# Two transformer blocks in one kernel: key and query products issued by array shape, and expert weights loaded one matrix at a time

## The chip, the core and the metric

The kernel runs on one core of a Trainium2 chip. The metric is the device time of one execution, in microseconds. Before the change it is 2284.15 us, the median of three runs (2281.66 to 2285.14).

In what follows PE is the matrix engine, DVE the vector engine, ACT the scalar engine, POOL the GpSimd engine and SP the queue that issues the loads. A matmul keeps one operand (the weights, at most 128 rows by 128 columns) in the array and streams the other one past it. "64 rows" below means that the contraction runs over 64 partitions, so that the matmul uses half of the array's rows; "64 columns" means that its output has 64 partitions.

## What is computed

512 tokens of width 1024 go through two blocks, all in float32:

```python
# first block
h   = rms_norm(x, ln1_g);  proj = h @ w_in
attn = neighbourhood_attention(rms_norm(q), rms_norm(k), v, rpb)   # 8 heads of 64
dn   = bidirectional_gated_deltanet(...)                           # 4 heads of 128, both directions
x = x + concat(attn, dn) @ w_out
x = x + hierarchical_moe(rms_norm(x, ln2_g), ...)                  # 64 experts, 2 per token
# an expert:  hid = silu(xb @ w_gate[e]) * (xb @ w_up[e]);  out = hid @ w_down[e]

# second block
proj = rmsnorm(x) @ w_in_2
y = three branches: mlstm, short_conv, stick_breaking              # the last: 16 heads of 64
# stick_breaking, per head:
z = q @ k.T / 8;  log_beta = log_sigmoid(z);  log_1m = where(s < t, log_beta - z, 0)
a = where(s < t, exp(log_beta + log_1m.sum() - cumsum(log_1m)), 0);  out = a @ v
x = x + merged @ w_out;  x = x + relu(rmsnorm(x) @ w_up)**2 @ w_down
return rmsnorm(x)
```

## The kernel before

Most products go through jobs: a weight tile of 1 MB is loaded into ring A (two buffers), ACT and DVE split it into a high and a low half (lines 160 and 161), and PE multiplies (high, high), (high, low) and (low, high), 24 matmuls of 128 rows, 128 columns and 512 streamed columns a job (`fm_mm`, line 255). The profile prints such operands as f32 too; they take one pass, and a true float32 matmul takes two records, one for each half of its weights.

Where nothing else is said, the framework schedules each engine's order from its own costs. In the expert loop and in the stick-breaking stage PE's order is written out by hand (`manual_schedule`).

**Neighbourhood attention** (about 264 to 361 us of the span). `na_attn` goes over 4 blocks of queries and 4 pairs of heads; `na_pair` (line 727) does one pair. For each head `i` of the pair it takes one PSUM tile `na_l` from the pool `pacc` (four banks), multiplies q by k (line 743: 64 rows, 256 or 384 streamed columns, the first head on partitions 0 to 63, the second on 64 to 127), adds the mask through an identity matrix `idb` (line 747: 128 rows, bf16), and lets DVE add the bias and take the maximum (line 750). The pair's turn is cut by `yield`s, between which `pad` lets the chunked scan of the delta rule (`dn_scan`) go on.

**Experts** (about 477 to 965 us). `moe` goes over 32 pairs of experts. Loads are queued in the order of `moe_loads` into rings of 1 MB tiles (A, B, C, H, O), and each takes its tile when one is free. `ld_gu` (line 1150) fills one tile with half `h` of an expert's gate and up matrices: two loads of 512 KB, each partition reading 4 KB in a row. `ld_down` (line 1159) fills a tile with one load of 1 MB, 8 KB in a row. `gate_up` (line 1441) then runs 8 steps `k`; in each, for both experts (output columns 0 to 63 and 64 to 127 of the array), one matmul streams 512 columns, 256 of gate and 256 of up. Between its first and second half stand the products of the pair before with the down matrix (`dn_o`, line 1482); behind it come the gather of the next tokens (`g_ps`, line 1426), and at the start of a pair the transposes `h_ps` (line 1464). The string `"ggaaaaggaaaa"` runs four steps of `gate_up` ahead of the first release of two tiles.

**Stick breaking** (about 1041 to 1295 us). `sb_pair` (line 1858) does two heads, `e` = 0 and 1, eight times over, between the dense jobs. Scores lie in three PSUM banks a head, `z[e][0..2]`, six of the pool `pat`'s six; the four regions `REG` have 512, 384, 256 and 128 columns. Per region and head stand one matmul of 128 rows (line 1868: `K` holds a head's rounded keys twice, `Q` its queries' high and low halves) and one of 64 rows (line 1870: `Kl`, the rest of the keys, on partitions 0 to 63 for head 0 and 64 to 127 for head 1). Then the mask is added through `idr` (line 1875), ACT and DVE compute the logarithms, and triangular and all-ones constants (`ntri`, line 1904; `none`, lines 1908 to 1913) sum them up on PE. The output `po` (`sb_o`, line 1923) takes a seventh tile of the pool, and `split_y` (lines 1682 and 1683) copies it out through ACT and then DVE.

**Constants**: `oner` and `none` are one column of ones and minus ones, read 128 times over with step 0 (`b2_consts`, line 1681); `oner` serves the mLSTM heads.

Of the kernel before, what the change touches and what calls it, by code (L numbers as in the profile page):

```python
# [10 lines left out]
F32 = mybir.dt.float32  # L11
# [70 lines left out]
class Kern:  # L82
# [648 lines left out]
    def na_pair(self, cb, g, block, po, sm):  # L731
# [4 lines left out]
        v = lambda a: a.rearrange("p (r k) -> p r k", r=8)  # L736
        for i in range(2):
            h = 2 * g + i
            hp, o = h // 2, 64 * (h % 2)
            lp = na.tile([128, 384], F32, name="na_lp", tag="na_lp", bufs=3)[:, :nb * 128]  # L740
            pl = self.pacc.tile([128, 384], F32, name="na_l", tag=self.atag)[:, :nb * 128]

            TE.matmul(pl, self.qT[o:o + 64, hp, cb, :],
                      self.kT[o:o + 64, hp, kb0 * 128:(kb0 + nb) * 128]
                      .rearrange("p (n r k) -> p r n k", n=nb, r=8), start=True, stop=False)
            mk = self.mk[:, None, s0:s0 + st * (nb - 1) + 1:st, :].to_broadcast([128, 8, nb, 16])
            TE.matmul(pl, self.idb, mk, start=False, stop=True)
            base = self.braw[:, h, 16 * (kb0 - cb + 1):16 * (kb0 - cb + 1) + 1]
            bias = bass.AP(tensor=base.tensor, offset=base.offset, ap=[list(base.ap[0]), [31, 8], [1, 16 * nb]])
            VE.tensor_tensor_reduce(out=v(lp), in0=v(pl), in1=bias, scale=1.0, scalar=NEG,  # L750
                                    op0=OP.add, op1=OP.max, accum_out=mx[:, i:i + 1])
            lps.append(lp)
            if i == 0:
                yield 0.3 * nb
# [395 lines left out]
    def ld_gu(self, t, e, h):  # L1150

        for i, nm in enumerate(("gate", "up")):
            src = self.A["expert_w_" + nm][e]
            if len(src.shape) == 3:
                src = src.rearrange("o r c -> (o r) c")
            self.SY.dma_start(t.rearrange("p (i j c) -> p i j c", i=2, j=4)[:, i],
                              src.rearrange("(p j) c -> p j c", j=8)[:, 4 * h:4 * h + 4, :])
# [6 lines left out]
    def moe_loads(self):  # L1164
        us = []
        for p in range(33):
            if p:
                us += [lambda t, e=2 * p - 2 + e: self.ld_down(t, e) for e in range(2)]
            if p < 32:
                us += [lambda t, e=2 * p + e, h=h: self.ld_gu(t, e, h) for h in range(2) for e in range(2)]  # L1170
# [271 lines left out]
    def gate_up(self, pool, xt, pp, w):  # L1442
# [3 lines left out]
        for k in range(8):  # L1446
            for e in range(2):
                o = pp * 128 + e * 64
                TE.matmul(pg[64 * e:64 * e + 64, :], xt[k // 4][:, k % 4, o:o + 64],  # L1449
                          w[k // 4 * 2 + e].rearrange("p (i j c) -> p i j c", i=2, j=4)[:, :, k % 4, :],  # L1450
                          start=(k == 0), stop=(k == 7))
            if k < 7:
                yield
# [50 lines left out]
    def moe(self):  # L1504
# [14 lines left out]
        with tc.manual_schedule(engines={mybir.EngineType.PE}):  # L1519
            hd, adds = None, iter(())  # L1520
            for p in range(33):
# [20 lines left out]
                for n in "ggaaaaggaaaa":  # L1542
# [649 lines left out]
```

## Time and profile before

| | |
|---|---|
| median of three runs | 2284.15 us (2281.66 to 2285.14) |
| profiled execution | 2290.18 us, of which 2288.4 us are the span of the trace |
| PE busy | 2196.5 us, 96% of the span, 11333 matmul records |
| DVE, ACT, POOL busy | 999.3, 783.0, 146.0 us |
| moved by DMA | 348.71 MB, 152 GB/s over the span; 405 GB/s between 515 and 944 us |

A row of a list of windows gives the stretch in us from the start of the span, its length, the busy time and the count of instructions of PE, of PE's weight loads (PEld), DVE, ACT and POOL, then the granted PE clock (1.00 is full), the busy share of the 16 DMA engines, and GB/s. A row of the timeline gives start, length, engine, line, operation, what is written from what, and the shape: "64*128 64x512" is 64 rows, 128 columns, 512 streamed columns. Matmuls are pipelined, so the time that one takes in a stream is read from start to start, not from its length. In a list of one line's instructions the three numbers are the shortest, the median and the longest in ns.

### The profile page before, as it was taken

Reading aid. Unit: us, or ns where it says so; the run is one execution under the profiler, and the core shown is the slowest. Engines: PE = TensorE matmul, PEld = TensorE weight load, DVE = VectorE, ACT = ScalarE, POOL = GpSimd, SP = SyncE. Lnnn points to the kernel's source line nnn. Section 1 sums busy time; section 2 is a strip of 40 time slices with the busy share of each in tenths; the row PEclk is TensorE's granted clock in tenths of the full one; section 3 lists DMA queues with packets and bytes.
Section 4 is the critical chain, followed back from the end, with each engine's and each line's share of the span. In section 5 each row is a group of like instructions: output and inputs, shape, how many; then the busy total and the mean of one; then the engine's idle time right before and its main releaser. Section 6 shows DMA issues by size and latency. Waiting matters only on the chain.

```text
span 2288.4 us, 27538 instructions
## 1 busy us (share of the span) xinstructions
PE 2196.5 (96%) x11333; PEld 1659.2 (73%) x11333; DVE 999.3 (44%) x1622; ACT 783.0 (34%) x1245; POOL 146.0 (6%) x171
## 2 busy tenths in 40 slices
PE   6989999899999999779999999999999999999998
PEld 4867787755555555357777788888888888888887
DVE  5479667521111111253555444555344444534333
ACT  3545543211111111134565524444322342423222
POOL 1020001000000000011122000000000000000000
PEclk9999999999999999888999999999999999999999
DMA  6212100789999999912111222222233322323322
GB/s 186 73 57 74 57 2 19 268 283 413 412 410 412 399 394 409 351 56 63 56 43 51 74 75 79 81 79 74 92 102 99 104 92 83 111 92 98 105 92 74
DMA packets 175397, 348.71 MB, mean 152 GB/s; under 512 B 15604, under 2 KB 115037, under 8 KB 167075
## 3 DMA queue, kind: packets, MB, share of 16 engines
q1 hardware_dynamic: 169827, 339.25, 41.6%
q0 software_dynamic: 4592, 4.50, 0.6%
q10 hardware_dynamic: 848, 3.15, 0.4%
q8 instruction: 91, 1.49, 0.3%
q14 instruction: 39, 0.32, 0.0%
HBM read 336.61 MB, written 22.02 MB: 157 GB/s over the span
## 4 chain that ended last, share of the span: by engine, by line
PE 56%; DVE 1%; ACT 0%; issue 0%; DMA 0%; POOLq 0%; POOL 0%; ACTq 0%
PE acc L255 37%; PE acc L305 8%; PE acc L332 2%; PE acc L214 2%; PE sb_z L1870 1%; PE sb_z L1868 1%; PE sb_o L1923 1%; PE sb_z L1904 1%; PE ml_s L2045 1%; PE ml_pn L2065 1%; PE pv L1825 0%; PE sb_z L1908 0%; PE n_ps L443 0%; PE sb_z L1875 0%; PE ml_pd L2065 0%; PE sb_z L1912 0%
## 5 line engine op out<-in xcount | busy, mean ns | idle before, releaser
L255 PE MATMUL acc<-hT,hl_fm 128*128 128x512 f32 x3504 | 829.9, 396 | 2.1 <-DVE hl_fm L161 2.0
L255 PEld LDWEIGHTS acc<-hT,hl_fm 128*128 128x128 f32 x3504 | 660.7, 190 | 142.8 <-issue 3.8
L161 DVE TENSOR_TENSOR hl_fm<-rawA,hl_fm 128x1024 fp32r<-128x1024 f32 x176 | 217.4, 1235 | 145.8 <-ACT hl_fm L160 145.6
L160 ACT CAST hl_fm<-rawA 128x1024 fp32r<-128x1024 f32 x176 | 184.6, 1050 | 269.4 <-PE acc L255 201.1
L1449 PE MATMUL gu<-rawB,XT 128*64 128x512 f32 x528 | 186.2, 609 | 12.8 <-DMA rawB<-in_expert_w_up_dram 12.5
L305 PE MATMUL acc<-hl_tm,uT 128*128 128x512 f32 x672 | 152.8, 389 | 0.0
L305 PEld LDWEIGHTS acc<-hl_tm,uT 128*128 128x128 f32 x672 | 126.1, 188 | 26.2
L1457 DVE TENSOR_TENSOR hd<-sg,gu 128x256 f32<-128x256 f32 x32 | 13.5, 421 | 274.8 <-ACT sg L1455 274.8
L1426 PEld LDWEIGHTS g_ps<-oneh,h 128*128 128x128 f32 x960 | 115.5, 188 | 23.6 <-issue 16.2
L1426 PE MATMUL g_ps<-oneh,h 128*128 128x256 f32 x960 | 121.7, 284 | 0.0
L1449 PEld LDWEIGHTS gu<-rawB,XT 128*64 128x64 f32 x528 | 57.9, 139 | 82.6 <-issue 72.2
L1485 ACT ACTIVATE obs<-dn_o,slots 128x512 f32<-128x512 f32 x60 | 41.2, 687 | 194.5 <-PE dn_o L1482 188.1
L1482 PE MATMUL dn_o<-rawB,ht 128*64 128x512 f32 x280 | 102.3, 605 | 1.6 <-DVE x L1501 1.6
L1449 PE MATMUL gu<-rawH,XT 128*64 128x512 f32 x208 | 94.3, 596 | 1.3 <-DMA rawH<-in_expert_w_up_dram 0.8
L161 DVE TENSOR_TENSOR hl_tm<-rawA,hl_tm 128x1024 fp32r<-128x1024 f32 x48 | 58.8, 1224 | 67.2 <-ACT hl_tm L160 67.1
L255 PE MATMUL acc<-yA,hl_fm 128*128 128x512 f32 x384 | 87.4, 389 | 0.0
L255 PEld LDWEIGHTS acc<-yA,hl_fm 128*128 128x128 f32 x384 | 72.1, 188 | 15.0
L160 ACT CAST hl_tm<-rawA 128x1024 fp32r<-128x1024 f32 x48 | 50.3, 1048 | 95.2 <-PE acc L305 86.4
L305 PE MATMUL acc<-hl_tm,hT 128*128 128x512 f32 x288 | 74.6, 413 | 0.0
L1449 PE MATMUL gu<-rawC,XT 128*64 128x512 f32 x152 | 70.5, 605 | 1.2 <-DMA rawC<-in_expert_w_up_dram 1.1
L305 PEld LDWEIGHTS acc<-hl_tm,hT 128*128 128x128 f32 x288 | 55.5, 198 | 11.1
L1440 ACT ACTIVATE XT<-g_ps,g 128x256 f32<-128x256 f32 x64 | 26.8, 470 | 106.0 <-PE g_ps L1426 100.6
(511 smaller groups left out, 2931.6 us busy)
## 6 DMA issues: line engine op xcount, KB each, us to landing
rawA<-in_w_in_dram SPq DMA_DIRECT2D x66, 1024.0 KB
rawB<-in_expert_w_down_dram SPq DMA_DIRECT2D x35, 1024.0 KB
rawB<-in_expert_w_gate_dram SPq DMA_DIRECT2D x66, 512.0 KB
rawB<-in_expert_w_up_dram SPq DMA_DIRECT2D x66, 512.0 KB
rawA<-in_w_up_dram SPq DMA_DIRECT2D x16, 1024.0 KB
rawA<-in_w_down_dram SPq DMA_DIRECT2D x16, 1024.0 KB
rawH<-in_expert_w_down_dram SPq DMA_DIRECT2D x13, 1024.0 KB
rawH<-in_expert_w_gate_dram SPq DMA_DIRECT2D x26, 512.0 KB
```

The source lines that it names most:

```text
L160: self.SE.copy(hi, src)
L161: self.VE.tensor_sub(lo, src, hi.bitcast(F32))
L214: self.TE.matmul(p[:, t:t + 256], j[4][:, a, k, :], h[:, b, k, t:t + 256], start=(t == 0 and i == 0), stop=(t > 0 and i == 23), skip_group ...
L255: self.TE.matmul(ps, hl[:, a, k, :], h[:, b, k, :], start=(n == 0), stop=(n == 23))
L305: self.TE.matmul(ps, h[:, a, k, c * 128:(c + 1) * 128], hl[:, b, kk, :], start=(first and n == 0), stop=(last and n == 5))
L332: self.TE.matmul(ps, h[:, a, k, c * 128:(c + 1) * 128], st["w"][:, b, k, :], start=(n == 0), stop=(n == 23))
L1426: TE.matmul(ps[:, k % 2, :], self.h2[:, a, c, k * 128:(k + 1) * 128], oh[:, c].rearrange("p e s -> p (e s)"), start=(n == 0), stop=(n == 7))
L1440: self.SE.activation(xt[:, 2 + j, :], ps[:, j, :], AF.Copy, scale=self.g2[:, 2 * i + j:2 * i + j + 1])
L1449: TE.matmul(pg[64 * e:64 * e + 64, :], xt[k // 4][:, k % 4, o:o + 64], w[k // 4 * 2 + e].rearrange("p (i j c) -> p i j c", i=2, j=4)[:, :, ...
L1482: TE.matmul(po[64 * e:64 * e + 64, :], ht[:, j, 64 * e:64 * e + 64], w[e].rearrange("p (j c) -> p j c", j=2)[:, j, s], start=(j == 0), sto ...
L1485: SE.activation(ob[:, s], po, AF.Copy, scale=sl[:, 1:2])
L1868: TE.matmul(z[e][b][:, c:c + n], K[:, e, ks], Q[:, e, i * 128:512], start=(i != 3), stop=False, skip_group_check=True)
```

## The change

It edits four places. In `na_pair` both heads' q by k products are issued first and both masks after them, with one `yield` behind both instead of one between the heads. In `sb_pair` the eight matmuls of 128 rows come first and the eight of 64 rows after them. `ld_gu` loads one whole matrix, gate or up, with one load of 1 MB (8 KB in a row for each partition), and `gate_up` runs 16 steps of 256 streamed columns, the 8 of gate ahead of the 8 of up. `oner` and `none` become full tiles of 128 by 128.

```diff
+        pls = [self.pacc.tile([128, 384], F32, name="na_l", tag=self.atag)[:, :nb * 128] for _ in range(2)]
+        for i in range(2):
+            o = 64 * i
+            TE.matmul(pls[i], self.qT[o:o + 64, g, cb, :],
+                      self.kT[o:o + 64, g, kb0 * 128:(kb0 + nb) * 128]
+                      .rearrange("p (n r k) -> p r n k", n=nb, r=8), start=True, stop=False)
+        for i in range(2):
+            TE.matmul(pls[i], self.idb, mk, start=False, stop=True)
...
-            if i == 0:
-                yield 0.3 * nb
+        yield 0.3 * nb
...
-    def ld_gu(self, t, e, h):
-        for i, nm in enumerate(("gate", "up")):
...
-            self.SY.dma_start(t.rearrange("p (i j c) -> p i j c", i=2, j=4)[:, i],
-                              src.rearrange("(p j) c -> p j c", j=8)[:, 4 * h:4 * h + 4, :])
+    def ld_gu(self, t, e, nm):
+        src = self.A["expert_w_" + nm][e]
+        self.SY.dma_start(t, src.rearrange("(p j) c -> p (j c)", j=8) if len(src.shape) == 2
...
-        for k in range(8):
+        for m, k in [(m, k) for m in range(2) for k in range(8)]:
             for e in range(2):
                 o = pp * 128 + e * 64
-                TE.matmul(pg[64 * e:64 * e + 64, :], xt[k // 4][:, k % 4, o:o + 64],
-                          w[k // 4 * 2 + e].rearrange("p (i j c) -> p i j c", i=2, j=4)[:, :, k % 4, :],
-                          start=(k == 0), stop=(k == 7))
+                TE.matmul(pg[64 * e:64 * e + 64, m * 256:(m + 1) * 256], xt[k // 4][:, k % 4, o:o + 64],
+                          w[2 * m + e][:, k * 256:(k + 1) * 256], start=(m == 0 and k == 0),
+                          stop=(m == 1 and k == 7), skip_group_check=True)
...
-                for n in "ggaaaaggaaaa":
+                for n in "ggggaaaaggggaaaa":
...
-        oner = p.tile([128, 1], F32R, name="oner")
-        self.oner = oner.to_broadcast([128, 128])
+        self.oner = r("oner", lambda t: VE.tensor_copy(t, self.ones), F32R)
...
             for e in range(2):
+                TE.matmul(z[e][b][:, c:c + n], K[:, e, i * 128:i * 128 + 128], Q[:, e, i * 128:512],
+                          start=(i != 3), stop=False, skip_group_check=True)
+
+        for i in range(4):
+            b, c, n = self.REG[i]
+            for e in range(2):
                 o = slice(64 * e, 64 * e + 64)
-                ks = slice(i * 128, i * 128 + 128)
-                TE.matmul(z[e][b][:, c:c + n], K[:, e, ks], Q[:, e, i * 128:512],
-                          start=(i != 3), stop=False, skip_group_check=True)
-                TE.matmul(z[e][b][:, c:c + n], Kl[o, ks], Q[o, e, i * 128:512],
+                TE.matmul(z[e][b][:, c:c + n], Kl[o, i * 128:i * 128 + 128], Q[o, e, i * 128:512],
```

On PE, at the start of the first pair of heads of stick breaking, the order before is this (`sb_z_7938`, 7939 and 7940 are head 0's three banks, 7941 to 7943 head 1's).

```order
L1868 MATMUL sb_z_7938<-sb_Q_7919,sb_K_7920 128x512
L1870 MATMUL sb_z_7938<-sb_Q_7919,sb_Kl_7921 128x512
L1868 MATMUL sb_z_7941<-sb_Q_7919,sb_K_7920 128x512
L1870 MATMUL sb_z_7941<-sb_Q_7919,sb_Kl_7921 128x512
L1868 MATMUL sb_z_7939<-sb_Q_7919,sb_K_7920 128x384
L1870 MATMUL sb_z_7939<-sb_Q_7919,sb_Kl_7921 128x384
L1868 MATMUL sb_z_7942<-sb_Q_7919,sb_K_7920 128x384
L1870 MATMUL sb_z_7942<-sb_Q_7919,sb_Kl_7921 128x384
```

Every matmul of 128 rows is followed by one of 64, sixteen times. After the change, at the middle of the same sixteen (head 0's banks are 8346 to 8348, head 1's 8349 to 8351):

```order
L1861 MATMUL sb_z_8348<-sb_Q_8327,sb_K_8328 128x256
L1861 MATMUL sb_z_8351<-sb_Q_8327,sb_K_8328 128x256
L1861 MATMUL sb_z_8347<-sb_Q_8327,sb_K_8328 128x128
L1861 MATMUL sb_z_8350<-sb_Q_8327,sb_K_8328 128x128
L1868 MATMUL sb_z_8346<-sb_Q_8327,sb_Kl_8329 128x512
L1868 MATMUL sb_z_8349<-sb_Q_8327,sb_Kl_8329 128x512
L1868 MATMUL sb_z_8347<-sb_Q_8327,sb_Kl_8329 128x384
L1868 MATMUL sb_z_8350<-sb_Q_8327,sb_Kl_8329 128x384
```

The sixteen now change their shape once inside, and the third bank of head 1 (8351) is first written by the sixth matmul instead of the eleventh.

On PE in neighbourhood attention, at one pair of heads with 384 columns, before (`na_o` is the product with v of the pair before, `sc_o` belongs to the scan):

```order
L743 MATMUL na_l_2583<-kv_90,qT_84 128x384
L747 LDWEIGHTS idb_89
L747 MATMUL na_l_2583<-bm_m_87,idb_89 128x384
L767 MATMUL na_pt_2587<-ident_114,na_e_2533 128x128 x3
L775 MATMUL na_o_2435<-kv_90,na_pT_2573 128x64 x3
L743 MATMUL na_l_2594<-kv_90,qT_84 128x384
L747 LDWEIGHTS idb_89
L747 MATMUL na_l_2594<-bm_m_87,idb_89 128x384
```

and after:

```order
L742 MATMUL na_l_2582<-kv_90,qT_84 128x384
L742 MATMUL na_l_2583<-kv_90,qT_84 128x384
L776 MATMUL na_o_2435<-kv_90,na_pT_2573 128x64 x3
L746 LDWEIGHTS idb_89
L746 MATMUL na_l_2582<-bm_m_87,idb_89 128x384
L746 LDWEIGHTS idb_89
L746 MATMUL na_l_2583<-bm_m_87,idb_89 128x384
```

The two products of 64 rows stand next to each other here. So they do in 9 of the 16 pairs (5 with 256 columns, 4 with 384); in the other 7 the schedule leaves matmuls of 128 rows between them.

On SP in the expert loop, the loads of one pair before, behind the down matrices of the pair ahead of it (the numbers tell tiles apart):

```order
L1161 DMA rawC_4033<-in_expert_w_down_dram 128x2048
L1161 DMA rawB_4035<-in_expert_w_down_dram 128x2048
L1156 DMA rawB_4153<-in_expert_w_gate_dram 128x1024
L1156 DMA rawB_4153<-in_expert_w_up_dram 128x1024
L1156 DMA rawH_4174<-in_expert_w_gate_dram 128x1024
L1156 DMA rawH_4174<-in_expert_w_up_dram 128x1024
L1156 DMA rawB_4177<-in_expert_w_gate_dram 128x1024
L1156 DMA rawB_4177<-in_expert_w_up_dram 128x1024
L1156 DMA rawB_4180<-in_expert_w_gate_dram 128x1024
L1156 DMA rawB_4180<-in_expert_w_up_dram 128x1024
```

and after:

```order
L1159 DMA rawA_4313<-in_expert_w_down_dram 128x2048
L1159 DMA rawC_4315<-in_expert_w_down_dram 128x2048
L1154 DMA rawC_4418<-in_expert_w_gate_dram 128x2048
L1154 DMA rawB_4420<-in_expert_w_gate_dram 128x2048
L1154 DMA rawB_4422<-in_expert_w_up_dram 128x2048
L1154 DMA rawH_4424<-in_expert_w_up_dram 128x2048
```

A pair's bytes and tiles stay the same; its loads go from ten to six, and PE's matmuls on them from 16 to 32 of half the width, in the same place between the other work.

More of the change, by code (lines that the diff above doesn't have):

```diff
@@ L736, in na_pair @@
         v = lambda a: a.rearrange("p (r k) -> p r k", r=8)
+        mk = self.mk[:, None, s0:s0 + st * (nb - 1) + 1:st, :].to_broadcast([128, 8, nb, 16])
+        pls = [self.pacc.tile([128, 384], F32, name="na_l", tag=self.atag)[:, :nb * 128] for _ in range(2)]
[6 more added lines that the diff above has]
+            TE.matmul(pls[i], self.idb, mk, start=False, stop=True)
         for i in range(2):
             h = 2 * g + i
-            hp, o = h // 2, 64 * (h % 2)
             lp = na.tile([128, 384], F32, name="na_lp", tag="na_lp", bufs=3)[:, :nb * 128]
[L741 to L747, printed above, removed]
             base = self.braw[:, h, 16 * (kb0 - cb + 1):16 * (kb0 - cb + 1) + 1]
             bias = bass.AP(tensor=base.tensor, offset=base.offset, ap=[list(base.ap[0]), [31, 8], [1, 16 * nb]])
-            VE.tensor_tensor_reduce(out=v(lp), in0=v(pl), in1=bias, scale=1.0, scalar=NEG,
+            VE.tensor_tensor_reduce(out=v(lp), in0=v(pls[i]), in1=bias, scale=1.0, scalar=NEG,
                                     op0=OP.add, op1=OP.max, accum_out=mx[:, i:i + 1])
             lps.append(lp)
-            if i == 0:
-                yield 0.3 * nb
+        yield 0.3 * nb
         VE.tensor_scalar(mx, mx, -1.0, None, op0=OP.mult)
@@ L1147, in dn_out @@
         VE.tensor_sub(self.yTd[:, 1, :, cs], sq, self.yTd[:, 0, :, cs].bitcast(F32))
-    def ld_gu(self, t, e, h):
-        for i, nm in enumerate(("gate", "up")):
-            src = self.A["expert_w_" + nm][e]
-            if len(src.shape) == 3:
-                src = src.rearrange("o r c -> (o r) c")
-            self.SY.dma_start(t.rearrange("p (i j c) -> p i j c", i=2, j=4)[:, i],
-                              src.rearrange("(p j) c -> p j c", j=8)[:, 4 * h:4 * h + 4, :])
+    def ld_gu(self, t, e, nm):
+        src = self.A["expert_w_" + nm][e]
+        self.SY.dma_start(t, src.rearrange("(p j) c -> p (j c)", j=8) if len(src.shape) == 2
+                          else src.rearrange("o (p j) c -> p (o j c)", j=8))
     def ld_down(self, t, e):
@@ L1169, in moe_loads @@
             if p < 32:
-                us += [lambda t, e=2 * p + e, h=h: self.ld_gu(t, e, h) for h in range(2) for e in range(2)]
+                us += [lambda t, e=2 * p + e, nm=nm: self.ld_gu(t, e, nm) for nm in ("gate", "up") for e in range(2)]
         for n, f in enumerate(us):
@@ L1609, in moe_rest @@
                         if n < 4:
-                            self.ld_gu(t, e, n // 2)
+                            self.ld_gu(t, e, ("gate", "up")[n // 2])
                         else:
@@ L1692, in b2_consts @@
         self.ntri = r("ntri", lambda t: VE.tensor_scalar(t, self.le, -1.0, None, op0=OP.mult), F32R, sb)
-        oner = p.tile([128, 1], F32R, name="oner")
-        VE.tensor_copy(oner, self.ones[:, 0:1])
-        self.oner = oner.to_broadcast([128, 128])
-        none = sb.tile([128, 1], F32R, name="none")
-        VE.tensor_scalar(none, self.ones[:, 0:1], -1.0, None, op0=OP.mult)
-        self.none = none.to_broadcast([128, 128])
+        self.oner = r("oner", lambda t: VE.tensor_copy(t, self.ones), F32R)
+        self.none = r("none", lambda t: VE.tensor_scalar(t, self.ones, -1.0, None, op0=OP.mult), F32R, sb)
         self.idr = r("idr", lambda t: VE.tensor_copy(t, self.ident))
```

2 lines of the change are left out of this document (1 added, 1 removed).

## Prediction

> **What bounds the kernel now.** I read the page first.
>
> ```profile
> span 2288.4 us, 27538 instructions
> PE 2196.5 (96%) x11333; PEld 1659.2 (73%) x11333; DVE 999.3 (44%) x1622; ACT 783.0 (34%) x1245; POOL 146.0 (6%) x171
> ...
> PEclk9999999999999999888999999999999999999999
> ```
>
> PE is busy for 96% of the span and no other engine for half of it. But a matmul counts as busy while it drains, so this row does not tell whether PE streams. I read each stage that the change touches from start to start in the timeline, and its resources from windows: attention (264 to 361), the expert loop where its loads run without a break (515 to 944), two short stretches of loads alone there, and the places in stick breaking where the clock fell.
>
> ```profile
> 264.00:361.00 97.00, 96.83 (x722) 77.58 (x718) 60.01 (x171) 42.46 (x124) 6.76 (x11) 1.00 0.04 12
> 515.00:944.00 429.00, 419.05 (x2226) 234.41 (x2222) 63.16 (x138) 73.89 (x140) 27.75 (x28) 1.00 1.02 405
> 518.00:521.00 3.00, 3.00 (x27) 2.87 (x25) 0.76 (x2) 0.07 (x1) 0.90 (x1) 1.00 1.01 423
> 524.00:530.00 6.00, 6.00 (x30) 2.01 (x28) 0.00 (x0) 0.79 (x2) 0.00 (x0) 1.00 1.02 406
> ```
>
> The last three numbers are clock, DMA share and GB/s. In attention DMA does nothing and PE does not rest: PE bounds it. In the expert loop the DMA engines are full (1.02) while PE rests for 10 us of 429. Which of the two sets the pace is read from the transposes `h_ps`, two at the start of each pair of experts; here for two stretches of the loop:
>
> ```profile
> L1464 PE MATMUL h_ps<-ident,hd x20: 270/272/275, 476.8 to 608.8; 128*128 128x128 f32 x20
> L1464 PE MATMUL h_ps<-ident,hd x24: 270/271/275, 623.5 to 798.8; 128*128 128x128 f32 x24
> ```
>
> The first ten pairs come every (608.8 - 476.8 - 0.1)/9 = 14.66 us, the next twelve every (798.8 - 623.5 - 0.1)/11 = 15.93 us, with the same matmuls in each. So 14.66 us is what PE needs and 15.93 us what the loads allow: at first PE eats a lead of tiles already loaded, and from about 609 us on the loop runs at the loads' pace, with 1.27 us of PE to spare per pair.
>
> **Stick breaking: the sixteen matmuls.** The timeline of the third pair of heads:
>
> ```profile
> 1107.30 0.47 PE L1868 MATMUL sb_z<-sb_Q,sb_K 128*128 128x512 f32 x1
> 1107.70 0.50 PE L1870 MATMUL sb_z<-sb_Q,sb_Kl 64*128 64x512 f32 x1
> 1108.13 0.50 PE L1868 MATMUL sb_z<-sb_Q,sb_K 128*128 128x512 f32 x1
> 1108.56 0.49 PE L1870 MATMUL sb_z<-sb_Q,sb_Kl 64*128 64x512 f32 x1
> ...
> 1112.48 0.32 PE L1870 MATMUL sb_z<-sb_Q,sb_Kl 64*128 64x128 f32 x1
> 1112.74 0.62 PE L1875 MATMUL sb_z<-m_le,idr 128*128 128x128 bf16 x8
> ```
>
> From 1107.30 to 1112.74 the block takes 5.44 us. The same eight widths in one shape, at full clock, stand a little later: the triangular sums of one head, followed by the sums with `none` and a dense matmul.
>
> ```profile
> 1125.53 1.38 PE L1904 MATMUL sb_z<-sb_hl,ntri 128*128 128x512 f32 x8
> 1126.75 0.56 PE L1908 MATMUL sb_z<-sb_hl,none 128*128 128x384 f32 x2
> ...
> 1127.84 0.61 PE L255 MATMUL acc<-hT,hl_fm 128*128 128x512 f32 x2
> ```
>
> Eight matmuls of 512, 512, 384, 384, 256, 256, 128 and 128 columns take 1.22 us, 0.48 ns a column. Two such sets would be 2.44 us; the block takes 3.00 more, for sixteen changes of shape: 0.19 us each. The same comes from single steps: 0.43 us where 512 columns stream in 0.24, and 0.26 where 128 stream in 0.06.
>
> After the change there are two changes of shape (0.4 us), the eight of 128 rows (1.22), and the eight of 64 rows. Those alternate between the array's upper and lower half and write different banks. If the halves work at once they take 1280 x 0.48 ns = 0.61 us, else 1.22. Nothing in this kernel runs 64 rows by 128 columns on both halves in turn; the nearest are the 64 by 64 products in the inversion of the delta rule, which alternate between halves of rows, and of columns too:
>
> ```profile
> 260.30 0.22 PE L1000 MATMUL p_m<-u,C 64*64 64x64 f32 x1
> 260.31 0.22 PE L1001 MATMUL p_m<-u,C 64*64 64x64 f32 x1
> 260.36 0.22 PE L1000 MATMUL p_m<-u,C 64*64 64x64 f32 x1
> ```
>
> Two start 0.01 us apart and the next 0.05 later, so they run at once, and I take 0.61. The new block is 1.22 + 0.4 + 0.61 = 2.23 us, a gain of 3.21; eight times, **25.7 us** (20.8 if the halves take turns). PE's order around the block is written out and stays, and ACT and DVE start on the scores when the block ends, as before. So their chain keeps its distance to the sums behind it, and the gain is PE's and the kernel's.
>
> One wait comes in. The third bank of head 1 is the one that held the `po` of the pair before. It is free when DVE has read it:
>
> ```profile
> 1106.99 0.58 ACT L1682 CAST yA<-sb_o 128x512 fp32r<-128x512 f32 x1 [1.97 <-PE sb_o L1923]
> 1107.58 0.69 DVE L1827 COPY sb_v<-pv 128x512 f32<-128x512 f32 x1 [3.04 <-PE pv L1825]
> 1108.19 0.68 DVE L1683 TENSOR_TENSOR yA<-sb_o,yA 128x512 fp32r<-128x512 f32 x1
> ```
>
> DVE ends at 1108.87. Before, this bank was wanted by the eleventh matmul, well past that; now by the sixth, 2048 x 0.48 ns = 0.98 us into the block, at 1108.28. It waits 0.6 us, and behind it in PE's queue the rest of the block. This is so where a group of two pairs begins with transposes (`pv`) and no dense job ahead, in pairs 3, 5 and 7: **minus 2 us** (0 to 4).
>
> **The clock in stick breaking.** The eight blocks, by the first and last start of their 64 matmuls of 128 rows, the clock over the whole stage, and five stretches with half the clock:
>
> ```profile
> L1868 PE MATMUL sb_z<-sb_Q,sb_K x64: 327/439/581, 1041.2 to 1269.3; 128*128 128x512 f32 x16, 128*128 128x384 f32 x16, 128*128 128x256 f32 x16, 128*128 128x128 f32 x16
> ...
> 1030.00:1300.00 270.00, 269.27 (x1267) 206.37 (x1266) 134.34 (x162) 149.00 (x235) 49.56 (x60) 0.96 0.17 52
> 1045.70:1052.50 6.80, 6.80 (x23) 5.37 (x24) 2.48 (x4) 5.27 (x9) 3.85 (x4) 0.50 0.00 0
> 1079.80:1086.60 6.80, 6.80 (x23) 5.08 (x23) 2.38 (x3) 3.60 (x7) 3.73 (x4) 0.50 0.00 1
> 1144.70:1148.10 3.40, 3.40 (x15) 2.80 (x16) 2.16 (x3) 3.08 (x6) 3.16 (x4) 0.50 0.02 5
> 1206.10:1209.50 3.40, 3.40 (x16) 2.78 (x16) 1.71 (x3) 2.57 (x6) 2.71 (x3) 0.50 0.01 2
> 1236.80:1240.20 3.40, 3.40 (x10) 2.62 (x9) 2.28 (x3) 3.40 (x8) 3.17 (x3) 0.50 0.00 0
> ```
>
> Together 23.8 us, in which 11.9 us of streaming are lost; that is the whole of what the stage's 0.96 leaves out (270 x 0.04 = 11). Each begins inside one of the eight blocks or right behind it, where PE streams for only 2.44 of 5.44 us; I read them as the throttle's answer to that. With a block of 2.2 us most should go. I take **9 us** of the 11.9 (bounds 0 and 12). The Trainium skill's page "TensorE: Matmul & The Clock Gate", in "Why this matters for your kernels", asks for no idle gaps of PE above some 3 us to keep the clock. Taken as the only cause, it would leave these halvings where they are, since PE is never idle for that long here, and the sum would be 39.7 instead of 48.7.
>
> **Attention.** Two rows of a head with 256 columns, and three with 384:
>
> ```profile
> 271.58 0.70 PE L743 MATMUL na_l<-kv,qT 64*128 64x256 f32 x2
> 272.21 0.28 PE L747 MATMUL na_l<-bm_m,idb 128*128 128x256 bf16 x1
> ...
> 291.56 0.34 PE L747 MATMUL na_l<-bm_m,idb 128*128 128x384 bf16 x1
> 291.83 0.91 PE L743 MATMUL na_l<-kv,qT 64*128 64x384 f32 x2
> 292.67 0.34 PE L747 MATMUL na_l<-bm_m,idb 128*128 128x384 bf16 x1
> ```
>
> A product takes 0.63 or 0.84 us. Where both heads' products now stand together (5 pairs of 256, 4 of 384) and the halves overlap, one of the two is hidden, and two changes of shape fall away, some 0.1 us net with what the second mask still needs: 5 x 0.73 + 4 x 0.94 = 7.4 us. In the 7 other pairs the changes are as many as before. Without overlap 0.9 us is left. DVE is busy for 60 of these 97 us, and the scan has a chain of its own that may show when PE gets shorter, so I take **6 us**.
>
> **Experts.** By the sizes of its packets the stretch 518 to 521 holds down matrices above all (8 KB in a row) and runs at 423 GB/s; 524 to 530 holds gate and up (4 KB) and runs at 406. From 515 to 944 us 429 x 405 GB/s = 174 MB are moved, two thirds of them gate and up, less some 4 MB of other loads: 112 MB. At 423 instead of 406 GB/s they take 112,000 KB x (1/406 - 1/423) = 11.1 us less; bounds 0 and 11, and since 3 us are a short stretch I take **10 us**. All of it counts, because the loads set the pace: a pair of experts would come every 15.5 us, still above the 14.66 that PE needs. SP, which now issues six loads instead of ten a pair, has nothing else queued behind them.
>
> PE pays for twice the matmuls of half the width. What 16 records of 512 columns cost, and 16 of 512, 384, 256 and 128 in the same shape (`sb_o`):
>
> ```profile
> 614.20 3.76 PE L1449 MATMUL gu<-rawB,XT 128*64 128x512 f32 x16
> 617.64 0.59 PE L1482 MATMUL dn_o<-rawC,ht 128*64 128x512 f32 x1
> ...
> 1072.57 2.37 PE L1923 MATMUL sb_o<-sb_t,sb_v 128*64 128x512 f32 x16
> 1074.88 0.50 PE L255 MATMUL acc<-hT,hl_fm 128*128 128x512 f32 x1
> ```
>
> 3.44 us for 8192 columns is 0.42 ns a column, 2.31 for 5120 is 0.45. So gate and up, 6.9 us a pair of experts, grow by 0.5 us at most, inside the 1.27 to spare; only if that cover were gone would it cost 32 x 0.5 = 16 us. I take 0. The constants: eight matmuls with `none` take 1.09 us for 2048 columns, 0.53 ns a column against 0.48 with a full tile and wider rows. If all of that were the step of 0, full tiles would save 0.1 x 16 = 1.6 us; the larger copies that build them cost less than that. I take 0.
>
> **Sum.** 25.7 - 2 + 9 + 6 + 10 = 48.7 us. The profiled execution took 2290.2 us (span 2288.4), 6 more than the median of the runs; against its own time it becomes 2241.5, against the median 2284.2 **2235 us**.
>
> **Rivals.**
> *The halves take turns* (chance 0.12): both heads' products of 64 rows stream one after the other. For it: no row shows this shape. Against it: `p_m`. It costs 4.9 us in stick breaking and 5.1 in attention: 38.7, 2245.
> *The clock falls all the same* (0.15), from something else in that stage. For it: three of the eight blocks have no halving, so the block alone does not decide. Against it: nowhere else between 1041 and 1295 us is there one. 39.7, 2244.
> *The loads don't get faster* (0.12): 406 and 423 are chance, and a run of 4 KB is as good as one of 8. For it: the two stretches are short. Against it: the whole stretch's 405 lies with the shorter runs, which are two thirds of it. 38.7, 2245. The page "DMA: Bandwidth & Descriptors" of the Trainium skill, in "Specifications", puts full line rate at 512 B and more, which would make these two alike; the two rows are against it so far.
> *PE's time is not passed on* (0.08): ACT and DVE, or the scan's chain, end last once PE is shorter. Half of the 34.7 us in stick breaking and all of attention would go: 25, 2259. For it: DVE's 60 of 97 us in attention; in stick breaking nothing.
> *Slower* (0.04): with 256 columns the weights of gate and up are no longer loaded behind the matmul ahead of them. Each of the 32 steps of two records a pair of experts pays the 0.19 us of a change of shape, or part of it. From 1.27/32 = 0.04 us a step on, PE overtakes the loads; at 0.14, three quarters of it, a pair takes 14.66 + 4.5 = 19.1 us, and the loop grows by 10 x 4.5 + 22 x 3.2 = 115 us, the whole by 115 - 38.7 = 76: 2360. Against it stands `sb_o`, at 0.45 ns a column with widths down to 128.
> The forecast itself has 0.49.
>
> **Range and chances.** The forecast's own terms at their ends, 20.8 to 25.7, 0 to 4 for the wait, 6 to 12 for the clock, 4 to 7.4, 7 to 11, reach from 2228 to 2250; with the first rivals, two of them together (2255), and a scatter of some us between runs I give 2220 to 2260. Faster by over 0.2%, about what can be told from no change here: 0.94 (the forecast, the first three rivals and three quarters of the fourth); within it 0.02; slower 0.04.
>
> **What would show it.** In the profile after: blocks of about 2.2 us from the first `sb_K` matmul to the first with `idr`, with pairs of `sb_Kl` starting together (2.8 and one by one if the halves take turns); no half clock between 1030 and 1300; a wait of about 0.6 us at the sixth matmul of three blocks; pairs of `na_l` products starting together; 418 GB/s or more in the expert loop, `h_ps` every 14.7 and then 15.5 us. The prediction is wrong if the blocks are short but the stage is not, or if the loop's period grows.

## The result, and the profile after

The changed kernel takes 2231.21 us, median of four runs (2230.98 to 2232.69); beside them the kernel before took 2282.9 (2278.37 to 2285.14). The ratio is 0.9777, 95% interval 0.976 to 0.9794: 51 us faster (47 to 55). The prediction was 2235 (2220 to 2260), faster. The profiled execution took 2231.41 us, 58.8 less than that of before; where the 8 us between the two differences come from is shown below.

The page of the changed kernel, with the same lines as of before and the packets of DMA (before there were 175397, of which 167075 under 8 KB):

```profile
span 2229.7 us, 29366 instructions
PE 2137.9 (96%) x12357; PEld 1681.0 (75%) x12357; DVE 999.2 (45%) x1622; ACT 783.7 (35%) x1245; POOL 140.9 (6%) x171
...
PEclk9999999999999999989999999999999999999999
...
DMA packets 156972, 348.82 MB, mean 156 GB/s; under 512 B 13556, under 2 KB 112989, under 8 KB 132259
```

PE is 96% busy as before, with 1024 more matmul records and 59 us less time: the share of busy time said nothing. Next the timeline of PE at the third and at the fourth pair of heads in stick breaking, start and length in us; in brackets the idle time ahead of a row and what ended it.

```profile
1071.42 1.17 PE L1861 MATMUL sb_z<-sb_Q,sb_K 128*128 128x512 f32 x5
1073.14 0.53 PE L1861 MATMUL sb_z<-sb_Q,sb_K 128*128 128x256 f32 x3 [0.54 <-DVE yA L1682]
1073.60 0.86 PE L1868 MATMUL sb_z<-sb_Q,sb_Kl 64*128 64x512 f32 x8
1074.39 0.62 PE L1873 MATMUL sb_z<-m_le,idr 128*128 128x128 bf16 x8
...
1101.18 1.38 PE L1861 MATMUL sb_z<-sb_Q,sb_K 128*128 128x512 f32 x8
1102.49 0.85 PE L1868 MATMUL sb_z<-sb_Q,sb_Kl 64*128 64x512 f32 x8
1103.27 0.62 PE L1873 MATMUL sb_z<-m_le,idr 128*128 128x128 bf16 x8
```

The fourth block takes 1103.27 - 1101.18 = 2.09 us, the third 2.97: its sixth matmul waits for DVE, as foretold. The whole stage is read from the first `sb_K` matmul to the last `sb_o` matmul, in the lists of these lines: `sb_o` before, then `sb_K` and `sb_o` after (the first start of `sb_K` before, 1041.2, stands in the prediction).

```profile
L1923 PE MATMUL sb_o<-sb_t,sb_v x128: 272/432/644, 1072.6 to 1293.5; 128*64 128x512 f32 x32, 128*64 128x384 f32 x32, 128*64 128x256 f32 x32, 128*64 128x128 f32 x32
```

```profile
L1861 PE MATMUL sb_z<-sb_Q,sb_K x64: 220/337/478, 1017.7 to 1211.3; 128*128 128x512 f32 x16, 128*128 128x384 f32 x16, 128*128 128x256 f32 x16, 128*128 128x128 f32 x16
```

```profile
L1921 PE MATMUL sb_o<-sb_t,sb_v x128: 272/432/644, 1042.8 to 1236.1; 128*64 128x512 f32 x32, 128*64 128x384 f32 x32, 128*64 128x256 f32 x32, 128*64 128x128 f32 x32
```

The stage went from 1293.5 - 1041.2 = 252.3 us to 1236.1 - 1017.7 = 218.4, 33.9 less. The windows of after: all of stick breaking, attention (first product to last), and the expert loop.

```profile
1006.00:1240.00 234.00, 231.64 (x1257) 189.14 (x1256) 134.45 (x161) 147.10 (x232) 44.81 (x60) 1.00 0.20 61
264.00:363.10 99.10, 97.29 (x776) 82.28 (x776) 64.69 (x191) 44.01 (x130) 6.79 (x11) 1.00 0.04 12
505.00:924.00 419.00, 409.70 (x3090) 267.27 (x3086) 63.12 (x138) 74.13 (x140) 27.30 (x28) 1.00 1.00 411
```

The clock in stick breaking is 1.00 throughout, where before it was 0.96. Attention takes 99.1 us; before, the same stretch ran from 264.7 to 368.7, 104.0. In the loop the pairs of `h_ps` show the pace; before in its steady part, then after in the first fifteen pairs and in its steady part:

```profile
L1464 PE MATMUL h_ps<-ident,hd x18: 270/270/275, 639.3 to 765.8; 128*128 128x128 f32 x18
```

```profile
L1463 PE MATMUL h_ps<-ident,hd x30: 270/272/275, 466.6 to 672.5; 128*128 128x128 f32 x30
```

```profile
L1463 PE MATMUL h_ps<-ident,hd x14: 270/271/275, 704.9 to 798.5; 128*128 128x128 f32 x14
```

After: (672.5 - 466.6 - 0.1)/14 = 14.70 us while PE sets the pace, (798.5 - 704.9 - 0.1)/6 = 15.58 where the loads do, against (765.8 - 639.3 - 0.1)/8 = 15.80 before. The whole loop, first to last `h_ps`, takes 477.5 us instead of 487.9.

So the profiled difference of 58.8 us is made of stick breaking 33.9, the loop 10.4, attention 4.9, and some 9.6 in the stretches between and around them: 4.6 between attention and the loop, 2.9 between the loop and stick breaking, 1.3 behind stick breaking, and 0.7 ahead of attention.

In the first of them the execution of before had four half-clock stretches (20.4 us), that of after two (6.8). This is not the change's: the kernels below that carry its stick-breaking, loads or constants edit alone take 102.0 to 103.5 us there, like after (103.5), and the one with the attention edit alone takes 108.1, like before (108.1).

The next two come with the change, although the prediction has no term for them. From the last `h_ps` to the first `sb_K` it is 76.5 to 78.1 us in the five profiles of this study that have the old loads and gate and up products, and 73.3 to 75.0 in the nine that have the new ones. The largest wait of PE in this stretch, behind the last `dn_o`, before and then after:

```profile
PE cb_l L1500 <- issue: 8.4, 1, 8.4
```

```profile
PE cb_l L1499 <- DMA bif<-in_b_if_dram: 5.4, 1, 5.4
```

It takes 8.4 to 8.8 us in the five profiles and 5.1 to 5.7 in the nine; why it is shorter stays open. From the last `sb_o` to the end it is 994.9 us in the five profiles with the old constants and 993.6 in the nine with full tiles. Only 0.1 us of the 1.3 is there when the last product with `oner` starts, and where the rest comes from stays open too.

### The profile page after: what moved, and what is told of

It is laid out like the page before. It is cut to its first block, busy times and chain, and to the rows that moved or that the text cites. A ratio compares the mean times of both kernels' runs of the same rounds, so it can differ in the third digit from the quotient of the medians.

```text
span 2229.7 us, 29366 instructions
## 1 busy us (share of the span) xinstructions
PE 2137.9 (96%) x12357; PEld 1681.0 (75%) x12357; DVE 999.2 (45%) x1622; ACT 783.7 (35%) x1245; POOL 140.9 (6%) x171
## 4 chain that ended last, share of the span: by engine, by line
PE 55%; DVE 1%; ACT 0%; issue 0%; DMA 0%; POOLq 0%; POOL 0%; ACTq 0%
PE acc L255 38%; PE acc L305 8%; PE acc L332 2%; PE acc L214 2%; PE sb_o L1921 1%; PE sb_z L1902 1%; PE ml_s L2043 1%; PE ml_pn L2063 1%; PE pv L1820 0%; PE sb_z L1861 0%; PE sb_z L1906 0%; PE sb_z L1868 0%; PE n_ps L443 0%; PE ml_pd L2063 0%; PE sb_z L1910 0%; PE sb_z L1873 0%
## 5 line engine op out<-in xcount | busy, mean ns | idle before, releaser
L1448 PE MATMUL gu<-rawB,XT 128*64 128x256 f32 x1056 | 180.6, 386 | 11.9 <-DMA rawB<-in_expert_w_gate_dram 9.2
L1448 PEld LDWEIGHTS gu<-rawB,XT 128*64 128x64 f32 x1056 | 105.7, 138 | 59.7 <-issue 12.1
L1448 PE MATMUL gu<-rawH,XT 128*64 128x256 f32 x416 | 95.0, 381 | 3.1 <-DMA rawH<-in_expert_w_gate_dram 1.7
L161 DVE TENSOR_TENSOR hl_tm<-rawA,hl_tm 128x1024 fp32r<-128x1024 f32 x48 | 58.8, 1225 | 67.4 <-ACT hl_tm L160 67.3
L1448 PEld LDWEIGHTS gu<-rawH,XT 128*64 128x64 f32 x416 | 55.3, 137 | 22.4 <-DMA rawH<-in_expert_w_up_dram 4.6
L1448 PE MATMUL gu<-rawC,XT 128*64 128x256 f32 x304 | 69.6, 381 | 0.6 <-DMA rawC<-in_expert_w_up_dram 0.6
```

The costliest lines, as they stand in the source:

```text
L161: self.VE.tensor_sub(lo, src, hi.bitcast(F32))
L1448: TE.matmul(pg[64 * e:64 * e + 64, m * 256:(m + 1) * 256], xt[k // 4][:, k % 4, o:o + 64], w[2 * m + e][:, k * 256:(k + 1) * 256], start=( ...
```

## The experiments

Ratios are against the kernel before, run beside them.

**The parts alone.** Four kernels, each with one edit of the diff on top of the kernel before.

> The kernel before with the new order of the sixteen products in stick breaking and nothing else. Theory (the terms of the prediction as they stand): 25.7 us from eight shorter blocks, 2 us given back to the wait for a bank, 9 to 12 us because the clock is no longer halved there; 33 to 36 us faster than before, and no half clock between 1030 and 1300 us. Rival 1 (the clock is halved by something else in this stage and it was one of the other parts that took it away): 24 us faster, with half-clock stretches left. Rival 2 (other engines' chains take part of it back once PE is shorter): blocks of 2.1 us in the trace, but 15 to 20 us faster in time.

> The kernel before with the new order of the attention products and nothing else. Theory: 5 to 7 us faster, because the loads of the experts start earlier along with the rest. Rival: the loads set the end of the expert loop and do not start earlier, so the loop only waits longer for them: 0 to 1 us faster, with the first transpose of the loop 5 to 7 us earlier and the last one at the place where it was.

> The kernel before with whole gate and up matrices per load, and twice the matmuls of half the width, and nothing else. Theory (runs of 8 KB move faster than runs of 4 KB): 9 to 11 us faster, the pair of experts every 14.7 us and later every 15.6 us. Rival (the loop gained in the changed kernel because it began earlier): 0 to 3 us faster, the later pairs every 15.9 us as before.

> The kernel before with full tiles for the two constants and nothing else. Theory: 0, within 1 us either way; the eight matmuls with the constant of minus ones take 1.09 us as before. Rival (reading a column 128 times over with step 0 slows the loads of weights): 2 to 4 us faster, with the eight matmuls at 1.0 us or less. If the four parts do not depend on each other, the four differences of this call add up to the 51.7 us of the whole change; if the sum is off by over 5 us, some of them share or block a gain.

| part | median us | ratio | us of 2283 |
|---|---|---|---|
| before | 2281.63 | | |
| stick breaking | 2247.36 | 0.9863 (0.9845 to 0.9881) | -31 (-27 to -35) |
| attention | 2277.52 | 0.9984 (0.9969 to 0.9999) | -4 (-0 to -7) |
| loads and gate/up | 2271.7 | 0.9957 (0.9942 to 0.9971) | -10 (-7 to -13) |
| constants | 2282.44 | 1.0003 (0.9982 to 1.0023) | +1 (-4 to +5) |

The medians differ from that of before by -34.3, -4.1, -9.9 and +0.8, together -47.5, against -51.7 for the whole; by the ratios it is -44 against -51. Within what these runs can tell the parts add up, but an interaction of some us would not be seen.

The loads alone gained what their theory said, with a pair of experts every 14.70 and later every 15.6 us. Attention alone gained 4 us where 5 to 7 were expected. Its rival, that the loop only waits longer, falls: from the first attention product the loop starts after 207.3 us instead of 212.1, with 20.4 us of half clock on the way in both, and it takes 485.1 us, no more than the 484.3 to 487.9 of the other loops with the old loads. Where the half clock on that way is 6.8 us, it is 202.5 to 202.6 us long in seven profiles with the edit and 206.0 to 207.5 in four without. So 3.4 to 4.9 us of this part reach the loop. With the constants alone, the eight sums with `none` take 1.10 us against 1.09.

**The clock in four profiles.** The kernels with attention, loads or constants alone have the old order in stick breaking. So there are four profiles of one and the same stage, and they differ in how often the clock was halved. Two of the stretches, attention alone and constants alone:

```profile
1072.60:1076.00 3.40, 3.40 (x15) 2.88 (x15) 2.25 (x3) 3.26 (x6) 3.24 (x4) 0.50 0.01 2
```

```profile
1163.70:1170.50 6.80, 6.80 (x23) 5.20 (x23) 2.38 (x3) 4.05 (x8) 3.85 (x4) 0.50 0.00 0
```

| old order, profile of | half clock in the stage, us | first `sb_K` to last `sb_o`, us |
|---|---|---|
| attention alone | 13.6 (4 stretches) | 248.0 |
| loads alone | 20.4 (5) | 251.0 |
| before | 23.8 (5) | 252.3 |
| constants alone | 30.6 (7) | 256.1 |

All 21 stretches begin inside one of the blocks of sixteen or less than 1 us behind one. The four times lie close to a line: (256.1 - 248.0)/(30.6 - 13.6) = 0.48 us for each microsecond at half clock, and 248.0 - 13.6 x 0.48 = 241.5 us without any. All ten profiles with the new order or with one shape, experiments below among them, have no half clock in this stage. With the new order it takes 218.4 us (218.0 with the stick-breaking edit alone). So by this line, of the 33.9 us, 252.3 - 241.5 = 10.8 are the clock's and 241.5 - 218.4 = 23.1 are PE's own. This settles the first expectation for its theory: the stick-breaking edit alone takes the half clock away and gains 34 us, and the other three parts leave it there.

**Is it the shape?** On the kernel before:

```diff
-                TE.matmul(z[e][b][:, c:c + n], Kl[o, ks], Q[o, e, i * 128:512],
+                TE.matmul(z[e][b][:, c:c + n], Kl[:, ks], Q[:, e, i * 128:512],
```

> The kernel before, with its old alternating order, but the eight products that used 64 rows now run over all 128 rows of Kl and Q (this adds the product of the other head's remainders to the scores, nothing is left out). So the order, the changes of weights and the banks are as before, and only the shape no longer changes. Theory (each change of shape costs 0.19 us): 5120 columns at 0.48 ns, blocks of 2.4 us instead of 5.4, no half clock in the stage, 33 to 37 us faster. Rival (it is the changes of weights and banks, or reading Kl at all, that cost): blocks of 5 us or more, no gain.

2248.51 us, ratio 0.9842 (0.9815 to 0.9868). The timeline of the third pair, old order, one shape:

```profile
1090.64 0.47 PE L1868 MATMUL sb_z<-sb_Q,sb_K 128*128 128x512 f32 x1
1090.96 0.39 PE L1870 MATMUL sb_z<-sb_Q,sb_Kl 128*128 128x512 f32 x1
1091.19 0.40 PE L1868 MATMUL sb_z<-sb_Q,sb_K 128*128 128x512 f32 x1
...
1093.24 0.62 PE L1875 MATMUL sb_z<-m_le,idr 128*128 128x128 bf16 x8
```

512 columns now take 0.23 us instead of 0.43, the block 2.60 instead of 5.44, and the stage 218.7 us: as short as with the new order, though nothing was moved. The eight products that the new order overlaps run one by one here, but there is neither a change of shape nor the wait. The changes of weights and banks, which stayed, are not what cost.

Then the size of one change. On the changed kernel:

```diff
         for i in range(4):
             b, c, n = self.REG[i]
             for e in range(2):
                 TE.matmul(z[e][b][:, c:c + n], K[:, e, i * 128:i * 128 + 128], Q[:, e, i * 128:512],
                           start=(i != 3), stop=False, skip_group_check=True)
-
-        for i in range(4):
-            b, c, n = self.REG[i]
             for e in range(2):
                 o = slice(64 * e, 64 * e + 64)
```

> The changed kernel with the sixteen products by regions: both heads' products of 128 rows, then both of 64 rows, four times. Eight changes of shape (seven inside the block) instead of two. Theory (0.19 us each, halves overlap, and the third bank of head 1 is wanted so late that nothing waits for it): 1.22 + 8 x 0.19 + 0.61 = 3.35 us a block, 26.8 us for eight against the 19.5 of the changed kernel, 7 us slower than it. The clock: if it is halved where too little streams, not or hardly here, since the block still streams for over half of its time. Rival (the shape costs a fixed time once per block, whatever the number of changes): blocks of 2.2 us.

2237.3 us, ratio 0.9798 (0.9771 to 0.9824). Its third pair:

```profile
1075.15 0.71 PE L1861 MATMUL sb_z<-sb_Q,sb_K 128*128 128x512 f32 x2
1075.79 0.50 PE L1865 MATMUL sb_z<-sb_Q,sb_Kl 64*128 64x512 f32 x2
1076.23 0.62 PE L1861 MATMUL sb_z<-sb_Q,sb_K 128*128 128x384 f32 x2
...
1078.53 0.62 PE L1870 MATMUL sb_z<-m_le,idr 128*128 128x128 bf16 x8
```

A block of 3.38 us where 3.35 was expected, no wait for the bank, and no half clock. The stage takes 225.7 us, 7.3 more than in the changed kernel; 0.19 us a change of shape holds.

**Do the halves work at once?** On the changed kernel, the products of 64 rows head by head:

```diff
-        for i in range(4):
-            b, c, n = self.REG[i]
-            for e in range(2):
+        for e in range(2):
+            for i in range(4):
+                b, c, n = self.REG[i]
                 o = slice(64 * e, 64 * e + 64)
                 TE.matmul(z[e][b][:, c:c + n], Kl[o, i * 128:i * 128 + 128], Q[o, e, i * 128:512],
```

> The changed kernel with the eight products of 64 rows issued head by head, the four of head 0 and then the four of head 1, so that neighbours use the same half of the array. Theory (the halves work at once only when neighbours use different halves): 1.22 us for these eight instead of 0.61, blocks of 2.7 to 2.8 us without the wait for the bank, 4 to 5 us slower than the changed kernel. Rival (a product of 64 rows is cheaper in any order): blocks and time as in the changed kernel.

The theory missed, and so did its reason. 2232.52 us, ratio 0.9777 (0.9754 to 0.9799), blocks of 2.10 and 2.97 as in the changed kernel. In the program head 0's 512, 384, 256 and 128 columns now stand ahead of head 1's 512. The list of this line over the first 0.3 us of the fourth pair's products:

```profile
L1868 PE MATMUL sb_z<-sb_Q,sb_Kl x2: 492/494/497, 1103.2 to 1103.2; 64*128 64x512 f32 x2
```

Two matmuls start there, and both have 512 columns: the fifth in the program starts with the first, ahead of three that stand before it. So order was no test of the halves. The next kernel takes one half away:

```diff
-                o = slice(64 * e, 64 * e + 64)
+                o = slice(0, 64)
                 TE.matmul(z[e][b][:, c:c + n], Kl[o, i * 128:i * 128 + 128], Q[o, e, i * 128:512],
```

> The changed kernel with both heads' products of 64 rows on the same 64 rows (partitions 0 to 63 of Kl and Q), in the order of the changed kernel; head 1 gets a wrong remainder of its keys by this. After head by head issue left the halves at work together, this takes the second half away. Theory (two halves at once are worth 0.6 us a block): the eight start one by one and take 1.2 us, blocks of 2.7 us where nothing waits, 5 us in all slower than the changed kernel. Rival (64 rows alone are cheaper, and the starts side by side in the trace only show how instructions are issued): blocks of 2.1 us as in the changed kernel.

2239.09 us, ratio 0.9812 (0.978 to 0.9844). Its fourth pair:

```profile
1102.58 1.38 PE L1861 MATMUL sb_z<-sb_Q,sb_K 128*128 128x512 f32 x8
1103.89 1.50 PE L1868 MATMUL sb_z<-sb_Q,sb_Kl 64*128 64x512 f32 x8
1105.32 0.62 PE L1873 MATMUL sb_z<-m_le,idr 128*128 128x128 bf16 x8
```

From the first `sb_Kl` to the first `idr` 1.43 us instead of 0.78 (1103.27 - 1102.49), a block of 2.74; the stage takes 223.5 us, 5.1 more. Two halves at once are worth 0.65 us a block.

**The wait for the bank.** On the changed kernel:

```diff
         if lo is None:
-            self.VE.tensor_copy(v, p)
+            self.SE.copy(v, p)
```

> The changed kernel with the copy of the transposed v (pv to sb_v) on ACT instead of DVE, so that DVE can read the output of the pair before, and free its bank, 0.7 us sooner. Theory (the wait at the sixth matmul of pairs 3, 5 and 7 is for this bank): the wait of 0.7 us goes or falls below 0.2, blocks of 2.1 to 2.3 us in all eight pairs, 2 to 2.5 us faster than the changed kernel. Rival (ACT, with 8 more copies of 0.6 us, is late for casts that PE waits for): the wait goes, but new waits of PE for ACT of 0.5 us or more stand in the stage, and the time is the same or longer.

DVE reads the pair before's output (`yA`) at the third pair of heads, first in the changed kernel, then here, and behind it PE's rows here:

```profile
1072.32 0.68 DVE L1682 TENSOR_TENSOR yA<-sb_o,yA 128x512 fp32r<-128x512 f32 x1
```

```profile
1076.42 0.69 DVE L1682 TENSOR_TENSOR yA<-sb_o,yA 128x512 fp32r<-128x512 f32 x1 [3.08 <-ACT yA L1681]
```

```profile
1076.11 1.62 PE L1861 MATMUL sb_z<-sb_Q,sb_K 128*128 128x512 f32 x8
1077.65 0.86 PE L1868 MATMUL sb_z<-sb_Q,sb_Kl 64*128 64x512 f32 x8
1078.45 0.62 PE L1873 MATMUL sb_z<-m_le,idr 128*128 128x128 bf16 x8
```

It starts 0.31 us into the block instead of 0.90, the blocks of pairs 3, 5 and 7 fall from 2.97 to 2.34, and the stage from 218.4 to 216.5 us. So the wait was for this bank. The one wait of PE that is left in the stage, 0.7 us at `pv`, is in the changed kernel too, so the rival, new waits for ACT, falls. In time the kernel is not told from the changed one: 2231.3 us, 0.9767 (0.9742 to 0.9792); 1.9 us is less than these runs resolve.

**What makes the loads faster.** Three forms of the load of one gate or up matrix, on the changed kernel (`s` is the matrix with 8 KB a partition). Two loads of 64 partitions:

```diff
...
+        for i in range(2):
+            self.SY.dma_start(t[64 * i:64 * i + 64], s[64 * i:64 * i + 64])
```

> The changed kernel with each gate or up matrix in two loads of 512 KB, 64 partitions each, every partition still reading 8 KB in a row. Ten loads a pair of experts as before the change, with the runs of after. Theory (the length of the run sets the rate): nothing changes against the changed kernel, 418 GB/s in the loop, the later pairs every 15.6 us, time within 3 us of it. Rival (what helped was fewer and larger loads): 405 to 411 GB/s, the later pairs every 15.9 us, 8 to 10 us slower than the changed kernel.

Two loads of half a row:

```diff
...
+        for i in range(2):
+            self.SY.dma_start(t[:, 1024 * i:1024 * i + 1024], s[:, 1024 * i:1024 * i + 1024])
```

> The changed kernel with each gate or up matrix in two loads of 512 KB, all 128 partitions each, every partition reading 4 KB in a row. Theory (the length of the run sets the rate): the loop loses what it gained, 405 to 411 GB/s, the later pairs every 15.9 us, 8 to 11 us slower than the changed kernel. Rival (gate ahead of up, whole matrices per tile, is what helped): 418 GB/s, the later pairs every 15.6 us, time as in the changed kernel.

The first of them told nothing on the question: 2590.23 us, ratio 1.1321 (1.1271 to 1.1371), by far the largest effect in this study, foreseen by neither side. So the question was put once more, as one load:

```diff
+        self.SY.dma_start(t.rearrange("p (h w) -> p h w", h=2),
+                          src.rearrange("(h p j) c -> p h (j c)", h=2, j=4) if len(src.shape) == 2
...
```

> The changed kernel with each gate or up matrix in one load of 1 MB as there, but each partition now reads two runs of 4 KB (rows 4p to 4p+3 of the matrix's upper half and of its lower half) instead of one of 8 KB; the expert products then pair the wrong rows of the matrix with the tokens. This is the clean form of the question that the two loads of 64 partitions could not answer. Theory (the length of the run sets the rate): as with two loads of 4 KB runs, 403 to 408 GB/s in the loop, the later pairs every 15.8 us, 6 to 9 us slower than the changed kernel. Rival (the number and size of the loads set the rate): 418 GB/s, the later pairs every 15.6 us, time as in the changed kernel.

Windows 700 to 800 of before, after, two loads of 64 partitions, two loads of 4 KB runs, one load of 4 KB runs:

```profile
700.00:800.00 100.00, 97.96 (x520) 57.57 (x521) 15.06 (x35) 16.41 (x32) 6.36 (x7) 1.00 1.01 405
```

```profile
700.00:800.00 100.00, 98.69 (x733) 64.45 (x731) 14.63 (x33) 17.15 (x33) 6.76 (x7) 1.00 1.01 419
```

```profile
700.00:800.00 100.00, 70.87 (x439) 45.85 (x436) 7.06 (x15) 9.56 (x18) 3.85 (x4) 0.82 1.01 234
```

```profile
700.00:800.00 100.00, 98.17 (x727) 63.37 (x727) 14.35 (x32) 16.42 (x32) 6.38 (x7) 1.00 1.02 406
```

```profile
700.00:800.00 100.00, 98.77 (x734) 64.30 (x730) 14.57 (x33) 17.09 (x34) 6.74 (x7) 1.00 1.02 411
```

The last two numbers are the share in which the DMA engines are busy, always full, and GB/s. Two loads of 4 KB runs: 406 GB/s, 2239.05 us, ratio 0.9806 (0.9777 to 0.9834). One load of 4 KB runs: 411 GB/s, 2239.25 us, 0.9813 (0.9792 to 0.9833). Steady pairs of experts, two loads of 4 KB runs and then one:

```profile
L1465 PE MATMUL h_ps<-ident,hd x12: 270/272/276, 718.2 to 797.4; 128*128 128x128 f32 x12
```

```profile
L1464 PE MATMUL h_ps<-ident,hd x10: 270/272/275, 736.2 to 799.5; 128*128 128x128 f32 x10
```

(797.4 - 718.2 - 0.1)/5 = 15.82 us and (799.5 - 736.2 - 0.1)/4 = 15.80, the pace of before, though tiles, order of matrices and matmuls are those of the changed kernel. The whole loop takes 486.3 and 484.7 us, against 477.5. With runs of 4 KB the gain is gone whatever the number of loads. Whether two loads instead of one cost the other 1.6 us stays open: loops with the loads of before took 484.3 to 487.9 us in five profiles.

Two loads of 64 partitions keep the DMA engines full at 234 GB/s. A pair of experts now comes every 28 us on average (25 to 33), PE waits for weights, and its clock falls to 0.82. The Trainium skill's page "SBUF — State Buffer", section "Door 1: The DMA port swizzle (why [64,N] ≈ [32,N])", says that partitions 0 to 63 reach only half of the 16 ports by which DMA writes, and 64 to 127 the other half. That agrees with 234 against 419 GB/s: the two thirds of the bytes that are gate and up at half of 419, and the rest at all of it, would make 251, an estimate from the 419. These runs show the rate and not the ports.

## Why the prediction was right, point by point

*The block of sixteen matmuls, 25.7 us less 2 for the wait* (23.7): 23.1. Blocks of 2.10 and 2.18 us were forecast as 2.23, changes of shape at 0.19 us hold, the halves do work at once. The 23.1 rests on the line through four profiles. The wait was forecast at 0.6 us in pairs 3, 5 and 7; it is 2.97 - 2.18 = 0.79 against the first pair's block, 2.4 us in all, of which the experiment above took 0.63 a block away.

*The clock, 9 us of 11.9*: all stretches went, and 10.8 us with them by the line above. The 11.9 was near, and the 3 us that the prediction held back for stretches that stay were not needed: the term was too small by 2. The rival that the clock falls all the same is out. What the throttle answers to is shown only so far: blocks of 5.4 us that change shape sixteen times bring it on, blocks of 3.4 us with eight changes and of 2.6 with none do not. PE was busy for 269.27 of the 270 us around this stage and for 6.80 of 6.80 in these stretches, so that the rule on idle gaps in the Trainium skill's page "TensorE: Matmul & The Clock Gate", section "Why this matters for your kernels", taken as the only cause, would have kept this term at 0; the runs decide against that reading.

*Attention, 6 us*: 4.9 in the stretch itself (104.0 us in all five profiles without the edit, 99.1 in all nine with it), and 3.4 to 4.9 up to the start of the loop. The mechanism was right: in all nine pairs where the products stand together they run at once. But PE now rests for 99.10 - 97.29 = 1.8 us there. Its waits in this stretch, before and after (total, times, longest in us):

```profile
PE na_py L793 <- DVE na_at L790: 0.2, 1, 0.2
```

```profile
PE na_py L794 <- DVE na_at L791: 1.3, 3, 0.6
PE na_pt L768 <- ACT na_e L760: 0.3, 1, 0.3
```

So the fourth rival, that other engines end last once PE is shorter, holds for some 1.5 us of this term, and for little in stick breaking, where PE rests for 234.00 - 231.64 = 2.4 us, 1.6 of them (3 x 0.54) in the waits for the bank.

*Loads, 10 us*: 10.4 by the two profiles; the mean of five loops with the old loads (486.3) and of six with the new (477.7) gives 8.6. The forecast of 15.5 us a pair and of 418 GB/s was met with 15.58 and 419 where the loads set the pace; from 505 to 924 us it is 411, since PE sets the pace for the first fifteen pairs. A pair in the steady part gains only 15.80 - 15.58 = 0.22 us. Much of the gain lies in the pairs from the eleventh to the fifteenth, which now come at PE's 14.70. The two short stretches, 423 against 406, gave the right size; over 100 us it is 419 against 405. The Trainium skill's page "DMA: Bandwidth & Descriptors", "Specifications", puts line rate at 512 B and more; here runs of 8 and of 4 KB differ by 2 to 3%, and that is 8 to 10 us of this kernel.

*PE's doubled matmuls, 0, and the constants, 0*: 14.70 against 14.66 us where PE sets the pace, 0.04 us a pair under the bound of 0.5, and hidden behind the loads afterwards. The slower rival, weights that are no longer loaded behind a matmul, did not come. The constants left the sums with `none` as they were; the 1.3 us behind stick breaking that come with them are less than the runs of that part alone resolve (-4 to +5).

The forecast of 48.7 us compares with 23.1 + 10.8 + 4.9 + 10.4 = 49.2 measured by stage, and with 51.7 in the medians. Each term was near because it was read from starts in the stage where it acts. That the sum is so near is in part luck: the clock was taken 2 us too small and attention 1 us or more too large, and the 2.9 and 1.3 us that the change gained outside these stages stood in no term. With them the stages make 53.4.

## What to carry to other kernels

Read matmuls from start to start and compare with the same width in an unbroken stream: a PE that is 96% busy lost 3 of 5.4 us to changes between 128 and 64 rows, and in such blocks the clock was halved as well. Grouping by shape and running all 128 rows took the same time here (218.0 and 218.7 us with nothing else changed), so take the one that moves less; for all 128 rows the half that doesn't belong to the product has to be zero, which the kernel above leaves out. Where loads set the pace, let each partition read one long run and let each load span all partitions; where they do not, look for the chain that PE will wait for next before counting all of PE's gain.

## What was not expected of the hardware

- Matmuls on different halves of the array's rows start together even when the program puts four of one half ahead of the other's (0.01 us apart, head by head).
- A load of 1 MB in two parts of 64 partitions costs 359 us of 2231 in this kernel, with the DMA engines shown as full at 234 GB/s.
- The same stage, unchanged, had 13.6 to 30.6 us of half clock from one profile to the next, 248.0 to 256.1 us. A single profile's clock is a draw; a term for it needs several.
